# Two-tensor GpSimd instructions cut into pieces of 256 columns, in a two-layer attention kernel on one core

## The chip, the core and the metric

The kernel runs on one NeuronCore of a Trainium2 chip, in one launch. Five engines work beside each other, each through its own list of instructions in order: TensorE (PE in the profile, with its weight loads as PEld), VectorE (DVE), ScalarE (ACT), GpSimd (POOL) and SyncE (SP), which here only issues DMAs. The metric is the device time of the launch in microseconds, the median over runs. One more run carried the profiler; the trace and all rows below are from that one.

## The reference

What is computed is a small transformer of two layers over 1024 image tokens of 1024 features and 256 context tokens, all in float32. The first layer has a windowed attention of 8 heads with a sink (A) and a differential attention of 4 heads (B). The second has a neighbourhood attention (D) and one with low-rank keys and values (M). Around them stand a modulated norm, the input projections with rotary position turns, a gate, the output projection and a last norm. The part that the change touches most is the differential attention, which takes the difference of two softmaxes:

```
def _diff_attend(q, k, v, lam):
    s = jnp.einsum('bqhte,bkhte->bhtqk', q, k).astype(jnp.float32) * (q.shape[-1] ** -0.5)
    p = jax.nn.softmax(s, axis=-1)
    a = (p[:, :, 0] - lam * p[:, :, 1]).astype(v.dtype)
    return jnp.einsum('bhqk,bkhe->bqhe', a, v)
...
    yb = rmsnorm(yb, b_subln_g) * (1.0 - lam_init)
```

## The kernel before

TensorE multiplies in the format float32r. To keep float32 accuracy, every operand x is held as a high part (x copied into float32r, by ScalarE) and a low part (x minus its high part), and a product is three matmuls: high by high, high by low, low by high (`mm3`, L286 to L288). The subtraction that makes a low part is one instruction with two tensors as inputs. Low parts of values that lie in PSUM, the matmul accumulator, are made by VectorE; those of values in SBUF, the working memory, mostly by GpSimd: weights (`wlo`, L233, 1024 columns each), projected heads after the rotary turn (`hl`, L212, 512 columns), the modulated input (`hE` L502, `hO` L465), the output weights (`woE`, `woO`, L823) and the gated attention output (`yl`, L841). GpSimd also does one product of the rotary turn (`rot`, L314).

The program runs through stages in this order: start (norm and first projections), e1, A (first attention, with projections of B's heads between its steps), B, outE (output projection of layer one, input of layer two), o1 (projections of layer two), D, M, outO. In stages A, B, D and M a `pipeline` weaves the steps of scores, values and norms of successive units with "fill" work, mostly projections, so that TensorE has work in between. The final order on each engine is set when the program is built, by a scheduler that places each instruction after those it depends on; the hardware then runs each engine's list in order, and semaphores hold an instruction until its inputs are there. The scheduler follows dependencies by column ranges: a reader of columns 0 to 255 waits only for what wrote these.

Stage B, where the change adds most pieces, works in units of two query blocks (i = 0, 1) of one head. For each block there are two score maps E_[0], E_[1] of 128 rows by 1280 columns (256 in a unit of context queries). VectorE brings scores from PSUM to SBUF (`evac`, L382), ScalarE takes the exponential (L888), VectorE forms a factor cc per row (L893, L894), and the mix E_[0] + cc * E_[1] is made by GpSimd for i = 0 and by VectorE for i = 1:

```
if i in POOL_MIX:
    G.tensor_scalar(E_[1][:, :ncol], E_[1][:, :ncol], cc, 1.0, ALU.mult, ALU.mult)
    G.tensor_tensor(E_[0][:, :ncol], E_[0][:, :ncol], E_[1][:, :ncol], ALU.add)
```

These are L896 and L897. TensorE then transposes the mix block by block (L927), two blocks of 128 columns to a step, and multiplies it with the values (L393 to L395). At the end of four query blocks `b_norm` normalises: a chain of small VectorE instructions of 2 or 4 columns (`evB` L959 and L960, then `rsqrt`, L188 to L201, each needing the one before), one product from PSUM (L963), and transposes back (L953, L969). Chains of the same kind stand in the other norms; stage A has a short one for its sink (`eA`, L760 to L763).

The functions that the diff touches and what calls them:

Of the kernel before, what the change touches and what calls it, by code (L numbers as in the profile page):

```python
# [96 lines left out]
def body(nc, tc, I, out, dbg=None):  # L97
# [82 lines left out]
    def f32(ap):  # L180
        return ap.bitcast(F32)
# [23 lines left out]
    def rstd_of(ss, n, width):  # L205
        v = tiny.tile([P, n], F32, tag=f"rv{n}", name="rv")
        V.tensor_scalar(v, ss, 1.0 / width, EPS, ALU.mult, ALU.add)
        return rsqrt(v, n)

    def split_to(dst_hi, dst_lo, src, psum=True):  # L210
        A.copy(dst_hi, src)  # L211
        (V if psum else lo_eng()).tensor_tensor(dst_lo, src, f32(dst_hi), ALU.subtract)  # L212

# [6 lines left out]
    class Weights:  # L220
# [5 lines left out]
        def load(self, srcs, width=D):  # L226
            hi = self.p.tile([P, self.maxk, width], F32R, tag="whi", name="whi", bufs=self.hi_bufs)
            lo = self.p.tile([P, self.maxk, width], F32R, tag="wlo", name="wlo", bufs=self.hi_bufs)
            for j, s in enumerate(srcs):
                raw = self.raw()  # L230
                SY.dma_start(raw[:, :width], s)
                A.copy(hi[:, j], raw[:, :width])  # L232
                lo_eng().tensor_tensor(lo[:, j], raw[:, :width], f32(hi[:, j]), ALU.subtract)  # L233
            return hi, lo
# [75 lines left out]
    def rope_split(tp, ps, n, cs, c0, hi, lo, rows=P):  # L310
        rot = tp.tile([P, 512], F32, tag="rot", name="rot")[:rows, :n]
        r = tp.tile([P, 512], F32, tag="rr", name="rr")[:rows, :n]
        V.stream_shuffle(rot, ps[:rows, :n], SHUF)  # L313
        G.tensor_tensor(rot, rot, cs[:rows, 1, c0:c0 + n], ALU.mult)  # L314
        V.tensor_tensor(r, ps[:rows, :n], cs[:rows, 0, c0:c0 + n], ALU.mult)
# [135 lines left out]
    def h_cols(tp, xns, layer, j, c0, h, hf_act=0, width=512):  # L451
        n = len(xns) * P
        for kt in range(NK):
# [9 lines left out]
            else:  # L463
                V.tensor_scalar(hf[:, :n], ps[:, :n], gs, sh, ALU.mult, ALU.add)
            (V if kt % 2 else G).tensor_tensor(lo, hf[:, :n], f32(hi), ALU.subtract)  # L465
            yield 0.45
# [28 lines left out]
    def shift_cols(tp, layer, j, c0, n, h):  # L495
        for kt in range(NK):
# [4 lines left out]
            A.copy(hi, hf[:, :n])  # L501
            (V if SH_V and kt % SH_V == 0 else G).tensor_tensor(lo, hf[:, :n], f32(hi), ALU.subtract)  # L502
            yield
# [311 lines left out]
    def fill_out_weights(rp, wo, src, bufs=2):  # L815
        for kt in range(NK):
            raw = rp.tile([P, D], F32, tag="wada", name="woraw", bufs=bufs)
            SY.dma_start(raw, src[:, kt * D:(kt + 1) * D])
            for c in range(2):
                cs_ = slice(c * 512, (c + 1) * 512)  # L820
                A.copy(wo[c][0][:, kt], raw[:, cs_])
                eng = V if WO_V and kt % WO_V == c else G
                eng.tensor_tensor(wo[c][1][:, kt], raw[:, cs_], f32(wo[c][0][:, kt]), ALU.subtract)  # L823
            yield WO_Y
# [8 lines left out]
    def y_part(t, src, gsrc, half, k0, k1, b):  # L833
# [6 lines left out]
        A.copy(yh[:, ks], o[:, ks])  # L840
        (V if YL_V and half == YL_V - 1 else G).tensor_tensor(yl[:, ks], o[:, ks], f32(yh[:, ks]), ALU.subtract)  # L841

# [4 lines left out]
    with ExitStack() as st:  # L847
# [4 lines left out]
        def b_scores(hd, grp, res):  # L852
# [17 lines left out]
            for i in range(2):  # L870
# [24 lines left out]
                if i in POOL_MIX:  # L895
                    G.tensor_scalar(E_[1][:, :ncol], E_[1][:, :ncol], cc, 1.0, ALU.mult, ALU.mult)  # L896
                    G.tensor_tensor(E_[0][:, :ncol], E_[0][:, :ncol], E_[1][:, :ncol], ALU.add)  # L897
                else:
# [685 lines left out]
```

## Time and profile before

| quantity | value |
|---|---|
| median of 3 runs | 1689.58 us (1688.39 to 1693.33) |
| the profiled run's own time | 1694.41 us |
| its span, first to last instruction | 1692.6 us, 1.8 us less than its time |
| TensorE matmul busy | 1599.0 us, 94% of the span |
| VectorE busy | 1117.1 us, 66% |
| ScalarE busy | 779.0 us, 46% |
| GpSimd busy | 468.1 us, 28%, in 390 instructions |
| mean granted TensorE clock | 0.986 of full speed |

Busy time of an engine is the time that its records cover. A record of VectorE or GpSimd that had to wait for a resource after it was begun counts as busy for the wait too, so that a small instruction can show a long record. The idle time in square brackets is that of the engine just before an instruction, and behind the arrow stands what ended it.

### The profile page before, as it was taken

The page shows a single profiled execution, that of the slowest core. Times are in us where ns is not written, and L with a number is a line of the kernel's source. Part 1 is how long each engine was busy: PE and PEld are TensorE (multiplying, and loading weights), DVE is VectorE, ACT ScalarE, POOL GpSimd, SP SyncE. Part 2 cuts the span into 40 slices and gives each one's busy share as a digit, 9 for nine tenths or more (in the row PEclk, how much of TensorE's full clock was granted, in tenths as well). Part 3 has the DMA queues.
Part 4 walks back from the last instruction along what each step waited for, and adds up shares of the span by engine and source line. Part 5 has one row for each costly group of instructions (what it writes and reads, how often), then busy time and mean ns, then how long its engine had stood idle before and what let it go on. Part 6 is the DMA issues. An engine that isn't in the chain of part 4 may idle for free. (4 is left out here: it accounts for less than half of the span.)

```text
span 1692.6 us, 26893 instructions
## 1 busy us (share of the span) xinstructions
PE 1599.0 (94%) x9506; PEld 1355.1 (80%) x9506; DVE 1117.1 (66%) x2964; ACT 779.0 (46%) x1590; POOL 468.1 (28%) x390
## 2 busy tenths in 40 slices
PE   6998999999999989998899999999999999999997
PEld 3687778888878778887677898889788887889886
DVE  4782229778759888887678546342676756656586
ACT  5442107666646555665333322222465645545421
POOL 0351125545433222232222102010232313322110
PEclk9999999999999999998999999999999999999999
DMA  7447773242263332223654614567865345321363
GB/s 294 168 121 229 233 223 95 82 147 82 70 210 109 101 100 97 88 76 106 208 162 155 187 58 122 156 193 227 212 172 159 104 136 187 113 82 63 101 217 100
DMA packets 157198, 242.99 MB, mean 144 GB/s; under 512 B 10348, under 2 KB 103432, under 8 KB 154376
## 3 DMA queue, kind: packets, MB, share of 16 engines
q1 hardware_dynamic: 152152, 227.91, 43.8%
q10 hardware_dynamic: 4576, 11.54, 1.8%
q0 software_dynamic: 336, 1.84, 0.3%
q8 instruction: 75, 1.23, 0.3%
q14 instruction: 59, 0.48, 0.1%
HBM read 163.50 MB, written 77.74 MB: 143 GB/s over the span
## 5 line engine op out<-in xcount | busy, mean ns | idle before, releaser
L286 PE MATMUL mmps<-hE,whi 128*128 128x512 f32 (+1 forms) x408 | 148.8, 365 | 1.7 <-DVE gg L371 1.0
L288 PE MATMUL mmps<-hE,wlo 128*128 128x512 f32 (+1 forms) x408 | 146.7, 360 | 0.0
L287 PE MATMUL mmps<-hE,whi 128*128 128x512 f32 (+1 forms) x408 | 146.1, 358 | 0.0
L888 ACT ACTIVATE sB_t<-sB_t,mB 128x1280 f32<-128x1280 f32 (+1 forms) x80 | 95.5, 1194 | 60.6 <-DVE sB_t L382 54.1
L233 POOL TENSOR_TENSOR wlo<-wraw,whi 128x1024 fp32r<-128x1024 f32 x30 | 72.2, 2406 | 182.8 <-ACT whi L232 143.9
L880 PE MATMUL sps<-kb,qb 128*128 128x512 f32 (+1 forms) x416 | 107.4, 361 | 7.1 <-DVE sB_t L382 5.8
L286 PEld LDWEIGHTS mmps<-hE,whi 128*128 128x128 f32 x408 | 77.7, 190 | 12.8 <-issue 2.5
L288 PEld LDWEIGHTS mmps<-hE,wlo 128*128 128x128 f32 x408 | 77.4, 190 | 10.3 <-issue 0.8
L382 DVE TENSOR_SCALAR_CACHE_REDUCE sB_t<-sps,mB 128x512 f32<-128x512 f32 (+1 forms) x128 | 78.1, 612 | 10.9 <-PE sps L880 8.7
L880 PEld LDWEIGHTS sps<-kb,qb 128*128 128x128 f32 x416 | 69.4, 191 | 19.1 <-DVE sB_t L382 9.7
L287 PEld LDWEIGHTS mmps<-hE,whi 128*128 128x128 f32 x408 | 77.6, 190 | 8.8
L1419 POOL TENSOR_SCALAR sM_t<-sM_t,sM 128x1280 f32<-128x1280 f32 x32 | 43.0, 1346 | 143.7 <-DVE sM L1418 112.9
L1320 POOL TENSOR_SCALAR sD_t<-sD_t,sD 128x640 f32<-128x640 f32 (+1 forms) x64 | 48.5, 780 | 104.8 <-ACT phd L211 28.6
L287 PE MATMUL mmps<-hO,whi 128*128 128x512 f32 (+1 forms) x192 | 74.9, 390 | 1.3 <-POOL hO L465 1.2
L286 PE MATMUL mmps<-hO,whi 128*128 128x512 f32 (+1 forms) x192 | 75.8, 395 | 0.0
L288 PE MATMUL mmps<-hO,wlo 128*128 128x512 f32 (+1 forms) x192 | 74.5, 388 | 0.0
L896 POOL TENSOR_SCALAR sB_t<-sB_t,cB 128x1280 f32<-128x1280 f32 (+1 forms) x20 | 23.4, 1171 | 179.8 <-DVE cB L894 66.8
L755 ACT ACTIVATE sA_t<-sA_t,mA 128x640 f32<-128x640 f32 (+2 forms) x80 | 59.6, 745 | 25.1 <-DVE sA_t L382 24.2
L765 POOL TENSOR_SCALAR sA_t<-sA_t,eA 128x640 f32<-128x640 f32 (+2 forms) x80 | 57.7, 743 | 42.1 <-DVE eA L763 23.2
L211 ACT CAST phm<-tps 128x512 fp32r<-128x512 f32 x80 | 45.7, 584 | 51.1 <-PE tps L1446 50.8
L314 POOL TENSOR_TENSOR rot<-rot,csE 128x512 f32<-128x512 f32 x26 | 36.1, 1389 | 115.6 <-DVE rot L313 100.0
L212 DVE TENSOR_TENSOR plm<-tps,phm 128x512 fp32r<-128x512 f32 x80 | 54.4, 689 | 19.5 <-ACT phm L211 19.5
(436 smaller groups left out, 5304.4 us busy)
## 6 DMA issues: line engine op xcount, KB each, us to landing
wraw<-w_e SPq DMA_DIRECT2D x26, 512.0 KB
wada<-w_ada_e SPq DMA_DIRECT2D x24, 512.0 KB
wada<-w_ada_o SPq DMA_DIRECT2D x24, 512.0 KB
wraw<-w_o SPq DMA_DIRECT2D x22, 512.0 KB
qb<-qk SPq DMA_DIRECT2D x76, 128.0 KB
qd_t<-qd SPq DMA_DIRECT2D x32, 256.0 KB
qk<-hl SPq DMA_DIRECT2D x10, 512.0 KB
vb<-vh SPq DMA_DIRECT2D x20, 256.0 KB
```

The costliest lines, as they stand in the source:

```text
L211: A.copy(dst_hi, src)
L212: (V if psum else lo_eng()).tensor_tensor(dst_lo, src, f32(dst_hi), ALU.subtract)
L233: lo_eng().tensor_tensor(lo[:, j], raw[:, :width], f32(hi[:, j]), ALU.subtract)
L286: T_.matmul(ps, lh, rh, start=first, stop=False)
L287: T_.matmul(ps, lh, rl, start=False, stop=False)
L288: T_.matmul(ps, ll, rh, start=False, stop=last)
L382: V.tensor_scalar(dst, ps, -scale, prev, ALU.mult, ALU.min, accum_out=acc)
L755: A.activation(St[:, :nl + L], St[:, :nl + L], AF.Exp, bias=mx, scale=-1.0, accum_out=ssum[:, i:i + 1])
L765: G.tensor_scalar(Ps[i][:, :nl + L], Ps[i][:, :nl + L], e[:, i:i + 1], 1.0, ALU.mult, ALU.mult)
L880: T_.matmul(ps[:, :n], Q[:, t, hl, i * P:(i + 1) * P], K[:, t, c0:c0 + n], start=hl == 0, stop=hl == 1)
L888: A.activation(St[:, :ncol], St[:, :ncol], AF.Exp, bias=mx, scale=-1.0, accum_out=s0g[:, si:si + 1] if t == 0 else ssum)
L1320: G.tensor_scalar(Ps[i][:, :w_], Ps[i][:, :w_], ssum[:, i:i + 1], 1.0, ALU.mult, ALU.mult)
```

## The change

A helper `tt` takes the place of direct two-tensor calls. For any engine but GpSimd it issues what was issued before. On GpSimd it cuts an instruction of more than 256 columns into pieces of 256 columns of the same tiles, issued one behind the other. The scale of stage B's mix on GpSimd (one tensor and a factor per row) is cut in the same way. What is computed, the engines and the buffers are the same. A GpSimd instruction of 1024 columns becomes four, one of 1280 becomes five, one of 512 two; those of 256 columns (`hO`, the context units) stay. GpSimd's list grows from 395 instructions to 718. Two two-tensor instructions that don't go through the helper (`wkr` L1103 and `xn` L1505) stay whole, and so do all one-tensor scalings of stages A, D and M (L765, L1320, L1419).

```diff
@@ -207,9 +207,19 @@
         V.tensor_scalar(v, ss, 1.0 / width, EPS, ALU.mult, ALU.add)
         return rsqrt(v, n)
 
+    def tt(eng, out_, a, b, op):
+        n, dims = out_.shape[1], len(out_.shape)
+        step = 256 if dims == 2 else 2
+        if eng is not G or n <= step:
+            eng.tensor_tensor(out_, a, b, op)
+            return
+        for c in range(0, n, step):
+            cs_ = slice(c, min(c + step, n))
+            eng.tensor_tensor(out_[:, cs_], a[:, cs_], b[:, cs_], op)
+
     def split_to(dst_hi, dst_lo, src, psum=True):
         A.copy(dst_hi, src)
-        (V if psum else lo_eng()).tensor_tensor(dst_lo, src, f32(dst_hi), ALU.subtract)
+        tt(V if psum else lo_eng(), dst_lo, src, f32(dst_hi), ALU.subtract)
 
     lo_cycle = {"n": 0, "engs": [G]}
...
@@ -311,7 +321,7 @@
         rot = tp.tile([P, 512], F32, tag="rot", name="rot")[:rows, :n]
         r = tp.tile([P, 512], F32, tag="rr", name="rr")[:rows, :n]
         V.stream_shuffle(rot, ps[:rows, :n], SHUF)
-        G.tensor_tensor(rot, rot, cs[:rows, 1, c0:c0 + n], ALU.mult)
+        tt(G, rot, rot, cs[:rows, 1, c0:c0 + n], ALU.mult)
         V.tensor_tensor(r, ps[:rows, :n], cs[:rows, 0, c0:c0 + n], ALU.mult)
         V.tensor_tensor(r, r, rot, ALU.add)
         split_to(hi, lo, r, psum=False)
...
@@ -893,8 +903,10 @@
                 V.reciprocal(cc, ssum)
                 V.scalar_tensor_tensor(cc, cc, nlam, s0g[:, si:si + 1], ALU.mult, ALU.mult)
                 if i in POOL_MIX:
-                    G.tensor_scalar(E_[1][:, :ncol], E_[1][:, :ncol], cc, 1.0, ALU.mult, ALU.mult)
-                    G.tensor_tensor(E_[0][:, :ncol], E_[0][:, :ncol], E_[1][:, :ncol], ALU.add)
+                    for c0 in range(0, ncol, 256):
+                        e1 = E_[1][:, c0:c0 + 256]
+                        G.tensor_scalar(e1, e1, cc, 1.0, ALU.mult, ALU.mult)
+                    tt(G, E_[0][:, :ncol], E_[0][:, :ncol], E_[1][:, :ncol], ALU.add)
                 else:
                     V.scalar_tensor_tensor(E_[0][:, :ncol], E_[1][:, :ncol], cc, E_[0][:, :ncol], ALU.mult, ALU.add)
                 Ps.append(E_[0])
```

The calls in `Weights.load` (L233), `h_cols` (L465), `shift_cols` (L502), `fill_out_weights` (L823) and `y_part` (L841) change in the way that the one in `rope_split` (L314) does.

The lists that come of it: on GpSimd, in the middle of stage B, a mix of a context unit (256 columns), one of a full unit, and the low part of a weight tile stand so before (`sB_t` are the score maps, `cB` the factor, `wraw` and `whi` the weight and its high part):

```order
L896 TENSOR_SCALAR sB_t<-sB_t,cB 128x256
L897 TENSOR_TENSOR sB_t<-sB_t 128x256
L896 TENSOR_SCALAR sB_t<-sB_t,cB 128x1280
L897 TENSOR_TENSOR sB_t<-sB_t 128x1280
L233 TENSOR_TENSOR wlo<-wraw,whi 128x1024
```

And so now, where lines 214 and 218 are the two calls in the helper and L908 is the scale:

```order
L908 TENSOR_SCALAR sB_t<-sB_t,cB 128x256
L214 TENSOR_TENSOR sB_t<-sB_t 128x256
L908 TENSOR_SCALAR sB_t<-sB_t,cB 128x256 x5
L218 TENSOR_TENSOR sB_t<-sB_t 128x256 x5
L218 TENSOR_TENSOR wlo<-wraw,whi 128x256 x4
```

The order of the work is the same here as everywhere on GpSimd; all five pieces of the scale come ahead of the five of the sum.

On TensorE, at the beginning of stage B, the first transposes of a full unit's mix (`tps` from `sB_t`) stand among scores (`sps`) and a projection (`mmps`) so before:

```order
L286 MATMUL mmps<-hE_134,whi 128x512
L880 MATMUL sps<-kb,qb 128x512 x2
L927 MATMUL tps<-consts,sB_t 128x128
L880 MATMUL sps<-kb,qb 128x512 x2
L927 MATMUL tps<-consts,sB_t 128x128
L287 MATMUL mmps<-hE_135,whi 128x512
```

And so now (L296, L297, L890 and L939 are the lines that were L286, L287, L880 and L927):

```order
L939 MATMUL tps<-consts,sB_t 128x128
L890 MATMUL sps<-kb,qb 128x512 x2
L939 MATMUL tps<-consts,sB_t 128x128
L296 MATMUL mmps<-hE_135,whi 128x512
L890 MATMUL sps<-kb,qb 128x512 x2
L297 MATMUL mmps<-hE_135,whi 128x512
```

The transposes stand two places earlier, since each now waits for one piece of the sum and not for all of it. Of TensorE's 9304 instructions 93 stand elsewhere than before, nearly all in this stretch at the beginning of stage B, and the lists of VectorE and ScalarE differ there and in two places of the start stage; SyncE's list is the same.

## Rows read from the trace of the kernel before

**Rows 1.** The page, busy time, share of the span and instructions of an engine.
```profile
PE 1599.0 (94%) x9506; PEld 1355.1 (80%) x9506; DVE 1117.1 (66%) x2964; ACT 779.0 (46%) x1590; POOL 468.1 (28%) x390
```

**Rows 2.** Busy us by engine in stage B (instructions), clock, DMA.
```profile
487.00:800.00 313.00, 290.96 (x1809) 251.50 (x1808) 266.74 (x822) 186.45 (x372) 89.58 (x49) 0.98 0.30 96
```

**Rows 3.** Timeline, stage B: start us, us, engine, line, operation, tiles [idle before <- releaser].
```profile
578.51 1.34 POOL L896 TENSOR_SCALAR sB_t<-sB_t,cB 128x1280 f32<-128x1280 f32 x1 [1.95 <-DVE rst L199]
579.00 0.85 DVE L200 SCALAR_TENSOR_TENSOR rst<-rst,evB 128x4 f32<-128x4 f32 x1
...
579.93 2.92 POOL L897 TENSOR_TENSOR sB_t<-sB_t 128x1280 f32<-128x1280 f32 x1
580.26 2.62 DVE L201 SCALAR_TENSOR_TENSOR rsy<-rst,rsy 128x4 f32<-128x4 f32 x1
...
584.23 0.63 PE L969 MATMUL tps<-consts,of 128*128 128x128 f32 x4 [2.18 <-DVE of L963]
```

**Rows 4.** Timeline, the last unit of stage B.
```profile
774.43 2.94 POOL L897 TENSOR_TENSOR sB_t<-sB_t 128x1280 f32<-128x1280 f32 x1
774.46 2.92 DVE L959 SCALAR_TENSOR_TENSOR evB<-s0g 128x4 f32<-128x4 f32 x1
...
779.50 0.69 PE L927 MATMUL tps<-consts,sB_t 128*128 128x128 f32 x4 [2.34 <-DVE plb L212]
```

**Rows 5.** Timeline, two more idle times of TensorE in stage B.
```profile
600.05 0.50 PE L880 MATMUL sps<-kb,qb 128*128 128x512 f32 x1 [1.96 <-DVE sB_t L382]
...
663.36 0.50 PE L880 MATMUL sps<-kb,qb 128*128 128x256 f32 x2 [1.34 <-DVE sB_t L382]
```

**Rows 6.** PE alone by stretch: start:end, us, busy (instructions), granted clock, DMA, GB/s.
```profile
585.40:588.80 3.40, 3.40 (x14) 0.51 0.38 154
...
780.00:783.40 3.40, 3.40 (x18) 0.50 0.00 0
```

**Rows 7.** GpSimd's groups by form: count | busy us, mean ns | idle before.
```profile
L233 POOL TENSOR_TENSOR wlo<-wraw,whi 128x1024 fp32r<-128x1024 f32 x30 | 72.2, 2406 | 182.8 <-ACT whi L232 143.9 <-PE sps L288 34.9 <-ACT ph L211 4.0
L897 POOL TENSOR_TENSOR sB_t<-sB_t 128x1280 f32<-128x1280 f32 x16 | 47.2, 2950 | 1.3
...
L212 POOL TENSOR_TENSOR hl<-rr,hl 128x512 fp32r<-128x512 f32 x23 | 30.8, 1339 | 23.6 <-ACT hl L211 22.1 <-DMA qd<-hl 1.5
...
L896 POOL TENSOR_SCALAR sB_t<-sB_t,cB 128x1280 f32<-128x1280 f32 x16 | 21.5, 1344 | 163.7 <-DVE cB L894 61.5 <-PE sps L880 29.1 <-ACT of L949 28.5
...
L897 POOL TENSOR_TENSOR sB_t<-sB_t 128x256 f32<-128x256 f32 x4 | 2.9, 734 | 0.3
...
L896 POOL TENSOR_SCALAR sB_t<-sB_t,cB 128x256 f32<-128x256 f32 x4 | 1.9, 480 | 16.1 <-DVE rsy L201 9.1 <-DVE cB L894 5.3 <-DVE evB L959 1.8
```

**Rows 8.** Timeline, beginning of outE: GpSimd instructions back to back.
```profile
804.93 1.69 POOL L823 TENSOR_TENSOR woE<-woraw,woE 128x512 fp32r<-128x512 f32 x1 [3.86 <-ACT woE L821]
805.39 1.26 DVE L188 TENSOR_SCALAR rsi<-evB 128x4 int32<-128x4 int32 x1
...
806.59 1.28 POOL L841 TENSOR_TENSOR yl<-o_in,yh 128x512 fp32r<-128x512 f32 x1
806.68 1.20 DVE L189 TENSOR_SCALAR rsi<-rsi 128x4 int32<-128x4 int32 x1
...
807.92 0.50 PE L288 MATMUL mmps<-woE,yl 128*128 128x512 f32 x1 [0.77 <-POOL yl L841]
```

**Rows 9.** Timeline, stage o1.
```profile
1053.87 1.90 POOL L314 TENSOR_TENSOR rot<-rot,csO 64x512 f32<-64x512 f32 x1 [3.56 <-DVE rot L313]
1054.55 4.11 DVE L315 TENSOR_TENSOR rr<-krt,csO 64x512 f32<-64x512 f32 x1
1055.73 2.38 POOL L233 TENSOR_TENSOR wlo<-wraw,whi 128x1024 fp32r<-128x1024 f32 x1
```

**Rows 10.** A VectorE line of stage A, count: duration ns min/median/max, first and last start us.
```profile
L760 DVE TENSOR_TENSOR eA<-small,mA x20: 151/162/1847, 258.1 to 461.6; 128x4 f32<-128x4 f32 x20
```

**Rows 11.** Timeline, stage o1, TensorE behind the wait of Rows 9.
```profile
1061.12 0.50 PE L286 MATMUL sps<-cq,wqk 128*128 128x512 f32 x1 [2.66 <-ACT wqk L211]
```

More of the change, by code (lines that the diff above doesn't have):

```diff
@@ L232, in load @@
                 A.copy(hi[:, j], raw[:, :width])
-                lo_eng().tensor_tensor(lo[:, j], raw[:, :width], f32(hi[:, j]), ALU.subtract)
+                tt(lo_eng(), lo[:, j], raw[:, :width], f32(hi[:, j]), ALU.subtract)
             return hi, lo
@@ L464, in h_cols @@
                 V.tensor_scalar(hf[:, :n], ps[:, :n], gs, sh, ALU.mult, ALU.add)
-            (V if kt % 2 else G).tensor_tensor(lo, hf[:, :n], f32(hi), ALU.subtract)
+            tt(V if kt % 2 else G, lo, hf[:, :n], f32(hi), ALU.subtract)
             yield 0.45
@@ L501, in shift_cols @@
             A.copy(hi, hf[:, :n])
-            (V if SH_V and kt % SH_V == 0 else G).tensor_tensor(lo, hf[:, :n], f32(hi), ALU.subtract)
+            tt(V if SH_V and kt % SH_V == 0 else G, lo, hf[:, :n], f32(hi), ALU.subtract)
             yield
@@ L822, in fill_out_weights @@
                 eng = V if WO_V and kt % WO_V == c else G
-                eng.tensor_tensor(wo[c][1][:, kt], raw[:, cs_], f32(wo[c][0][:, kt]), ALU.subtract)
+                tt(eng, wo[c][1][:, kt], raw[:, cs_], f32(wo[c][0][:, kt]), ALU.subtract)
             yield WO_Y
@@ L840, in y_part @@
         A.copy(yh[:, ks], o[:, ks])
-        (V if YL_V and half == YL_V - 1 else G).tensor_tensor(yl[:, ks], o[:, ks], f32(yh[:, ks]), ALU.subtract)
+        tt(V if YL_V and half == YL_V - 1 else G, yl[:, ks], o[:, ks], f32(yh[:, ks]), ALU.subtract)
     mark("B")
```

## The prediction

> **What bounds the kernel now.** I read the page's busy times first: TensorE's matmuls cover 94% of the span, GpSimd 28% [rows 1]. A change on GpSimd can therefore not win by shorter GpSimd work; it can only win or lose through the some 94 us in which TensorE stands idle (1692.6 - 1599.0). Second, the busy times by stretch: in stage B TensorE was busy 290.96 of 313.00 us, so 22.0 us of that idle time lie here, the most of any stage [rows 2]. Third, I went through the timeline of stage B at TensorE's longest idle times, and looked at what VectorE and GpSimd did just before.
>
> What the reader should see first is a pattern of ends. A GpSimd scale of 1.34 us runs from 578.51 to 579.85, and `rst` of L200, 4 columns wide, has a record that ends at 579.85 also. The sum L897 runs from 579.93 to 582.85, and L201, begun at 580.26, ends at 582.88 [rows 3]. L959 and its L897 do the same at 774.46 [rows 4]. Four columns are no work for 2.9 us: a two-input instruction of the same width on L760 has a median of 162 ns in 20, with one of 1847 [rows 10]. So a VectorE instruction that takes two operands from SBUF, or one of the `rsqrt` chain, waits for the GpSimd instruction that is running, up to its whole length. TensorE pays behind it: its idle time of 2.18 us at 584.23 ends on a VectorE result that follows L201 [rows 3], that of 2.34 us at 779.50 on one that follows L959 [rows 4], and there are more of 1.96 and 1.34 us [rows 5]. After the first two the granted clock falls to 0.51 and 0.50, the lower of the two levels (1.2 GHz), for 3.40 us each [rows 6]. In o1 the longest case stands: L315 at 1054.55 takes 4.11 us, through the rest of `rot` and a whole `wlo` [rows 9], and TensorE then is idle for 2.66 us [rows 11].
>
> **The change part by part. The cost on GpSimd.** A two-tensor piece of 256 columns takes 734 ns, a scale piece 480 ns (L897 and L896 in the context units) [rows 7]. From the counts and means of the same group: `wlo` 30 x (4 x 734 - 2406) = 15.9 us (33 such, with three tiles of the start, by this estimate 17); the sum of the mix 16 x (5 x 734 - 2950) = 11.5; its scale 16 x (5 x 480 - 1344) = 16.9; the instructions of 512 columns (the 23 `hl`, and `rot`, `yl`, `woE`, `woO`, `hE`: some 100) at 2 x 734 - 1339 = 0.13 each, 13. Together about 59 us, so GpSimd goes from 468 to some 527 us, 31%. I cost them at nothing on the path, except where TensorE waits for GpSimd, because GpSimd was idle 182.8 us before `wlo`s and 163.7 before scales, waiting for its inputs [rows 7]. That cover is gone at the beginning of outE, where `woE` and `yl` come back to back and TensorE waits 0.77 us for `yl` [rows 8]; some eight pieces in such chains at 0.13 each make 1.0 us more, between 0 and 3.
>
> **The mix.** All five scales now come ahead of five sums: the first piece of the mix is ready after 5 x 0.48 + 0.73 = 3.1 us instead of 1.34 + 2.95 = 4.3, the last after 6.1. TensorE takes two blocks of 128 columns, one piece, to a transpose step, and other matmuls stand between the steps; so the first step can start 1.2 us earlier, and the last is 1.8 us late but several steps away. I take 0 for it, between -3 and +5 (the 16 full mixes, a quarter of 1.2 us gained or 0.3 us lost each).
>
> **What VectorE gets back.** The trace has no train of pieces, but it has GpSimd instructions back to back with VectorE at their boundary: `rsi` of L188 waits for `woE` to 806.62, ends at 806.65 and L189 is begun at 806.68, though `yl` follows at 806.59. Then L189 waits out `yl` to 807.87 [rows 8]. So one waiting instruction gets through at each boundary, and the next waits again. A wait that was up to 2.95 us becomes one of at most one piece, 0.73. A chain of single instructions can however pay a piece per link. From the four idle times of stage B:
> - 584.23: L201 waits 0.73 at most and not 2.62, which is 1.89 less of an idle time of 2.18. I take 1.9.
> - 779.50: L959 the same, 2.92 - 0.73 = 2.19; but it is the head of a chain whose next links fall into the train, now 0.7 us longer. I take 1.5.
> - 1.96 and 1.34 us [rows 5]: half of each, 1.0 and 0.7, since chains follow there too.
>
> That is 5.1 us of 7.8. The other 14.2 us of idle time in B (22.0 - 7.8) are many short ones; some end on the mix or on a VectorE instruction behind GpSimd and some on neither. I take a quarter, 3.5 us, between 0 and a half. The two stretches of low clock cost half of their 3.4 us, 1.7 each, as the same matmuls would take half at the full clock; if the idle time ahead goes, the stretch should go. Three quarters of it: 2.5. In stage A, L760 with its worst of 1847 ns is the head of the short chain: I take 1.0 for the twenty. In o1, L315 would wait for one piece instead of a piece and a `wlo`: of 2.66 us of idle time 1.5, between 0 and all. Start, e1, D, M, outE and outO I put at 0: their GpSimd instructions are of 256 columns already, or not cut, or stand beside DMA waits. A VectorE instruction that now runs sooner can hold GpSimd up in turn: `woE` with 1.69 us beside the mean of 1.34 for 512 columns shows that it waits as well [rows 7, 8]; this is in the 1.0 above.
>
> Sum: -5.1 - 3.5 - 2.5 - 1.0 - 1.5 + 1.0 = -12.6 us. The profiled execution took 1694.41 us (span 1692.6 and 1.8 around it), so it would take 1681.8; it was 4.8 us above the median of 1689.58. On the median the sum gives 1677.0.
>
> What the Trainium skill says of this wait points the same way for a single instruction and leaves the train open. "SBUF — State Buffer", section "Who interferes with whom", gives VectorE and GpSimd one pair of ports under an exclusive lock; who issues first keeps it for its whole instruction, and a VectorE instruction with two SBUF inputs needs it. The trace agrees: 2.62 and 2.92 us of waiting to the end of an L897 [rows 3, 4].
>
> **Rivals.**
> *The train holds on as one.* If the next piece is begun before the one in hand has wholly ended, VectorE may not get in between. For it speaks L315: it was begun at 1054.55 during `rot`, and did not get in when `wlo` was begun at 1055.73, with `rot` ending at 1055.77 [rows 9]. Against it speak the boundary at 806.62 [rows 8] and that between L896 and L897, where L200 ended [rows 3]; in those, all tiles have 128 partitions, as all pieces of the mix and of `wlo` have, where `rot` in o1 has 64. If it holds, a wait lasts for the train: each of the 16 sums ends 0.72 us later (3.67 instead of 2.95), each `wlo` 0.53. If all 16 reach TensorE, 16 x 0.72 = 11.5 us are lost: 1701. It decides from the point at which a small instruction beside a mix lasts over 2.95 us.
> The Trainium skill has the rule that would bring it about: "GPSIMD Engine Reference", section "2.1 Instruction dispatch", says that consecutive GpSimd instructions are no barrier between its cores, each of which starts its share of the next as soon as it is through with the last. By that rule the ports would never be quite free inside a train; the boundary at 806.62 does not bear that out for 128 partitions.
>
> *A piece per link, no net change.* In a chain of a dozen dependent small instructions each waits for one piece. Then only the first wait shrinks, the train is 0.7 us longer, and the end of the chain is where it was. For it: L188 and L189 paid 1.26 and 1.20 us one after the other [rows 8]. Against it: at 580 only L201 stood behind the sum, the last link before the product [rows 3]. The gains at 584 and of o1 alone (1.9 + 1.5) less 1.0 and 2 lost in longer trains give -0.4: 1689.
>
> *Half comes back.* The waits shrink, but TensorE meets the next late thing, the exponentials or a DMA of `qb`, within the same step, and the clock stays as it is: 12.6 less 2.5 for the clock and half the rest, about -5: 1684.
>
> *The change does nothing to the order.* On TensorE only 93 instructions stand elsewhere, so a better or worse order by itself is no case here.
>
> **How the numbers follow.** Chances: the forecast (-8 to -20) 0.60; half comes back 0.15; no net change 0.17; the train holds 0.08. The time predicted is 1677. Within 0.3% (5 us), which is about what a measurement of this kernel can tell from no change, lie 1684.5 to 1694.6. Faster: 0.60 and half of "half comes back", 0.68. Same: the other half, 0.07, and 0.13 of "no net change", 0.20. Slower: 0.04 and 0.08, 0.12. Low end: all of the four idle times (7.8), half of the other 14.2, both stretches (3.4), 2.7 in o1 and 2 in A, 23 us: 1666. High end: 1691, which holds "no net change" and leaves the train out, and the worse part of the mix.
>
> **What would show it.** In the profile after: the records of L959, L201 and their like no longer than 0.9 us; GpSimd busy some 527 us; TensorE's idle time in B near 11 us instead of 22; clock at 1.0 where 585.4 and 780.0 stood; the krt product in o1 (L315) at some 1.5 us. It is wrong if small VectorE records last 3 us and more beside a mix (the train), if they come in rows of 0.7 with the idle times where they were (a piece per link), or if TensorE's waits for GpSimd at outE grow by more than 3 us.

## The result, and the profile after

The changed kernel takes 1678.63 us (median of 7 runs, 1673.38 to 1683.13), the kernel before 1697.79 us (7 runs, 1688.39 to 1708.29). The ratio is 0.990, interval 0.987 to 0.993: 1.0% or some 17 us faster. The forecast was 1677.0 us, 12.6 less than the median then known (1689.58). With the runs taken since, that median is 8.2 us higher, so the difference is the fairer measure of the forecast than the time: 12.6 us forecast, some 17 measured. The profiled span fell from 1692.6 to 1671.6 us; this execution took 1673.38 us, the fastest of the seven and 5.2 us below their median, so that differences between profiles come out larger than the change is.

First line of the page of the changed kernel, to be set beside [rows 1]:

```profile
PE 1592.2 (95%) x9506; PEld 1347.9 (81%) x9506; DVE 1083.9 (65%) x2964; ACT 778.5 (47%) x1590; POOL 537.6 (32%) x713
```

GpSimd is 69.5 us busier, VectorE 33.2 us less with the same 2964 records: those 33 us were waits inside records. TensorE does the same 9506 matmuls in 6.8 us less, at a mean granted clock of 0.990 instead of 0.986, and idles 14.2 us less (93.6 to 79.4).

To see where, I cut both traces at the same matmuls. These are five stages of the changed kernel (start, A, B, o1, M): start:end, us, then busy us of PE, PEld, DVE, ACT and POOL (instructions), clock, DMA share, GB/s.

```profile
0.00:142.40 142.40, 118.42 (x657) 86.08 (x657) 87.29 (x162) 64.45 (x109) 56.49 (x64) 0.95 0.53 182
...
260.30:487.50 227.20, 225.85 (x1336) 194.92 (x1335) 173.91 (x522) 143.49 (x330) 121.03 (x171) 1.00 0.37 117
487.50:790.00 302.50, 285.99 (x1809) 246.39 (x1807) 255.72 (x821) 186.40 (x371) 117.31 (x194) 1.00 0.31 99
...
949.80:1189.00 239.20, 235.24 (x1387) 210.08 (x1387) 104.36 (x281) 67.90 (x147) 35.27 (x45) 1.00 0.55 164
...
1385.90:1578.80 192.90, 188.03 (x1274) 168.52 (x1273) 125.73 (x317) 104.01 (x172) 59.23 (x52) 1.00 0.32 104
```

The same for a second profile of the kernel before, taken later to see what a stage varies by with nothing changed:

```profile
0.00:141.00 141.00, 118.20 (x656) 86.02 (x656) 93.00 (x162) 64.16 (x109) 48.13 (x37) 0.95 0.54 184
...
260.70:489.70 229.00, 225.64 (x1335) 194.81 (x1334) 176.53 (x522) 143.58 (x330) 114.23 (x120) 1.00 0.37 116
489.70:801.40 311.70, 290.18 (x1808) 250.37 (x1807) 266.50 (x821) 186.07 (x371) 89.36 (x48) 0.98 0.30 96
...
960.10:1205.40 245.30, 238.48 (x1386) 212.54 (x1385) 108.56 (x281) 68.03 (x147) 29.49 (x19) 0.99 0.54 159
...
1405.20:1601.30 196.10, 189.79 (x1274) 169.99 (x1273) 127.94 (x317) 104.03 (x172) 56.49 (x42) 0.99 0.30 100
```

Against this second profile B gains 9.2 us (10.4 against the first, cut at the same matmuls), o1 6.1, M 3.2 (5.2 against the first), A 1.8, and the start loses 1.4 (3.6 against the first). Not all of this is the change. In the kernels further down that have the changed kernel's text of o1 and M, o1 takes 239.2 to 242.5 us, which is below the 244.9 and 245.3 of the two profiles of before, but M takes 192.9 to 197.1, so M's 3.2 to 5.2 us are not clear of noise. TensorE's idle time in B, span less busy time, went from 21.5 to 16.5 us.

The waits themselves. Duration ns min/median/max of three small VectorE lines in the changed kernel (L201 of `rsqrt`, L770 the former L760, and the second `evB`, L972):

```profile
L201 DVE SCALAR_TENSOR_TENSOR rsy<-rst,rsi x30: 149/161/736, 12.0 to 1026.6; 128x2 f32<-128x2 f32 x20, 128x4 f32<-128x4 f32 x10
```
```profile
L770 DVE TENSOR_TENSOR eA<-small,mA x20: 150/162/656, 260.2 to 462.1; 128x4 f32<-128x4 f32 x20
```
```profile
L972 DVE SCALAR_TENSOR_TENSOR evB<-ssB,evB x12: 152/156/1071, 510.7 to 794.8; 128x4 f32<-128x4 f32 x8, 128x2 f32<-128x2 f32 x4
```

Where maxima were 2.62 and 2.92 us [rows 3, 4] and 1847 ns [rows 10], they are now a piece, 0.74 us at most. The exceptions are L199 once beside `wkr`, which stays whole (1.27 us), and L972, which comes back below. In o1 the wait of 4.11 us at L315, now L325, is 1.23, and TensorE's idle time behind it 0.94 instead of 2.66 [rows 9, 11]. Timeline of the changed kernel there:

```profile
1041.92 2.50 POOL L218 TENSOR_TENSOR rot<-rot,csO 64x256 f32<-64x256 f32 x2 [3.55 <-DVE rot L323]
...
1042.60 1.23 DVE L325 TENSOR_TENSOR rr<-krt,csO 64x512 f32<-64x512 f32 x1
...
1047.35 0.50 PE L296 MATMUL sps<-cq,wqk 128*128 128x512 f32 x1 [0.94 <-ACT wqk L221]
```

### The profile page after: what moved, and what is told of

Read it like the earlier page. It is cut to its first block, busy times and chain, and to the rows that moved or that the text cites. A ratio compares the mean times of both kernels' runs of the same rounds, so it can differ in the third digit from the quotient of the medians.

```text
span 1671.6 us, 27299 instructions
## 1 busy us (share of the span) xinstructions
PE 1592.2 (95%) x9506; PEld 1347.9 (81%) x9506; DVE 1083.9 (65%) x2964; ACT 778.5 (47%) x1590; POOL 537.6 (32%) x713
## 3 DMA queue, kind: packets, MB, share of 16 engines
q8 instruction: 75, 1.23, 0.3%
## 5 line engine op out<-in xcount | busy, mean ns | idle before, releaser
L296 PE MATMUL mmps<-hE,whi 128*128 128x512 f32 (+1 forms) x408 | 148.3, 364 | 2.0 <-DVE gg L381 1.3
L297 PE MATMUL mmps<-hE,whi 128*128 128x512 f32 (+1 forms) x408 | 145.7, 357 | 0.3 <-POOL hE L218 0.3
L218 POOL TENSOR_TENSOR wlo<-wraw,whi 128x256 fp32r<-128x256 f32 x120 | 90.2, 783 | 172.9 <-ACT whi L242 137.7
L890 PE MATMUL sps<-kb,qb 128*128 128x512 f32 (+1 forms) x416 | 106.9, 358 | 4.1 <-DMA kb<-kb 2.3
L908 POOL TENSOR_SCALAR sB_t<-sB_t,cB 128x256 f32<-128x256 f32 x84 | 38.6, 478 | 154.6 <-DVE cB L904 74.5
L296 PEld LDWEIGHTS mmps<-hE,whi 128*128 128x128 f32 x408 | 77.2, 189 | 12.9 <-issue 2.5
L392 DVE TENSOR_SCALAR_CACHE_REDUCE sB_t<-sps,mB 128x512 f32<-128x512 f32 (+1 forms) x128 | 78.3, 613 | 12.3 <-PE sps L890 9.7
L297 PEld LDWEIGHTS mmps<-hE,whi 128*128 128x128 f32 x408 | 77.0, 189 | 9.4 <-POOL hE L218 0.7
L890 PEld LDWEIGHTS sps<-kb,qb 128*128 128x128 f32 x416 | 68.8, 189 | 16.1 <-DVE sB_t L392 5.2
L297 PE MATMUL mmps<-hO,whi 128*128 128x512 f32 (+1 forms) x192 | 74.9, 390 | 1.7 <-POOL hO L214 1.6
L218 POOL TENSOR_TENSOR rot<-rot,csE 128x256 f32<-128x256 f32 x52 | 41.5, 819 | 108.2 <-DVE rot L323 93.3
L296 PE MATMUL mmps<-hO,whi 128*128 128x512 f32 (+1 forms) x192 | 75.9, 395 | 0.0
L298 PE MATMUL mmps<-hO,wlo 128*128 128x512 f32 (+1 forms) x192 | 74.5, 388 | 0.0
L765 ACT ACTIVATE sA_t<-sA_t,mA 128x640 f32<-128x640 f32 (+2 forms) x80 | 59.6, 746 | 25.6 <-DVE sA_t L392 24.8
L218 POOL TENSOR_TENSOR yl<-o_in,yh 128x256 fp32r<-128x256 f32 x36 | 30.9, 878 | 125.2 <-ACT yh L850 125.2
```

Of the source, the lines that this page charges most:

```text
L218: eng.tensor_tensor(out_[:, cs_], a[:, cs_], b[:, cs_], op)
L296: T_.matmul(ps, lh, rh, start=first, stop=False)
L297: T_.matmul(ps, lh, rl, start=False, stop=False)
L298: T_.matmul(ps, ll, rh, start=False, stop=last)
L392: V.tensor_scalar(dst, ps, -scale, prev, ALU.mult, ALU.min, accum_out=acc)
L765: A.activation(St[:, :nl + L], St[:, :nl + L], AF.Exp, bias=mx, scale=-1.0, accum_out=ssum[:, i:i + 1])
```

## The experiments

**The mix alone, and all but the mix.** The first cuts only the mix:

```diff
-        if eng is not G or n <= step:
+        if True:
...
-                    tt(G, E_[0][:, :ncol], E_[0][:, :ncol], E_[1][:, :ncol], ALU.add)
+                    for c0 in range(0, ncol, 256):
+                        e0, e1 = E_[0][:, c0:c0 + 256], E_[1][:, c0:c0 + 256]
+                        G.tensor_tensor(e0, e0, e1, ALU.add)
```

The second cuts all but the mix:

```diff
-                    for c0 in range(0, ncol, 256):
-                        e1 = E_[1][:, c0:c0 + 256]
-                        G.tensor_scalar(e1, e1, cc, 1.0, ALU.mult, ALU.mult)
-                    tt(G, E_[0][:, :ncol], E_[0][:, :ncol], E_[1][:, :ncol], ALU.add)
+                    G.tensor_scalar(E_[1][:, :ncol], E_[1][:, :ncol], cc, 1.0, ALU.mult, ALU.mult)
+                    G.tensor_tensor(E_[0][:, :ncol], E_[0][:, :ncol], E_[1][:, :ncol], ALU.add)
```

> Only the mix of stage B is cut (scale and sum in pieces of 256); all other GpSimd instructions are whole as before. Theory (VectorE waits for a running GpSimd instruction to its end, and shorter pieces shorten that wait): the 10.4 us that the changed kernel gained in B stay for the most part, the 5.8 us of o1 and 5.2 us of M go, the start loses nothing: 8 to 10 us under the kernel before, ratio 0.994 to 0.996; no VectorE instruction beside a mix above 0.9 us, but L315 in o1 near 4 us again and those beside a weight's low part near 2.4. Rival (the mix is ready by pieces, so that transposes start earlier): the same in B, ratio 0.994. This run doesn't tell the two apart; it sizes the mix against the rest.

> All is cut but the mix, whose scale and sum are whole as before. Theory of the VectorE waits: the sums of 2.95 us hold VectorE again, with records of 2.5 to 2.9 us in B, TensorE's idle time in B between 18 and 22 us; o1 and M keep their gains: 6 to 10 us under the kernel before, ratio 0.994 to 0.996. Rival (readiness of the mix by pieces is what pays): B back at 22 us idle, and no gain at the places where only VectorE waited, ratio 0.998 to 1.0.

Measured: mix alone 0.9972 (0.9956 to 0.9988), all but the mix 0.9936 (0.9915 to 0.9957). Together 0.9908, the whole change's 0.990: the parts add up, and the mix is the smaller. The mix alone fell short of its forecast (0.994 to 0.996); all but the mix did slightly better than its own, which was the same. Stage B in the two, same columns:

```profile
490.50:803.20 312.70, 291.61 (x1808) 251.67 (x1807) 261.24 (x821) 186.21 (x371) 114.51 (x176) 0.98 0.30 96
```
```profile
488.10:792.90 304.80, 286.15 (x1809) 246.40 (x1808) 262.87 (x821) 185.66 (x370) 93.77 (x66) 1.00 0.31 98
```

With the mix alone, B is as long as before, though VectorE's records shrank by some 5 us, so this profile doesn't show where the 0.28% comes from. The timeline of that kernel shows one reason: a small VectorE record that waits not for one piece but to the end of all five (512.34 + 3.50 = 515.84), and TensorE idle behind it.

```profile
512.34 3.50 POOL L911 TENSOR_TENSOR sB_t<-sB_t 128x256 f32<-128x256 f32 x5
513.68 2.17 DVE L974 SCALAR_TENSOR_TENSOR evB<-ssB,evB 128x2 f32<-128x2 f32 x1
...
516.51 0.90 PE L890 MATMUL sps<-kb,qb 128*128 128x256 f32 x3 [1.84 <-DVE sB_t L392]
```

Without the mix's cut B is 7 to 8 us shorter than in the two profiles of before, and 4 to 5 of that is TensorE's busy time. Its idle time of 2.20 us behind a whole sum is still there, and yet the clock stayed at 1.00, the upper level, behind it. First the timeline, then PE by stretch (busy us, clock, DMA share, GB/s):

```profile
580.17 2.63 DVE L201 SCALAR_TENSOR_TENSOR rsy<-rst,rsy 128x4 f32<-128x4 f32 x1
...
584.16 0.63 PE L979 MATMUL tps<-consts,of 128*128 128x128 f32 x4 [2.20 <-DVE of L973]
```
```profile
583.80:587.20 3.40, 3.04 (x21) 1.00 0.65 188
587.20:590.60 3.40, 3.40 (x25) 1.00 0.13 52
```

**The kernel before once more.**

> The kernel before, profiled a second time, to see what a stage and a low-clock stretch vary by with nothing changed. If the low clock behind the idle times at 582 and 777 us belongs to them, it is there again, and stage B takes 312 to 314 us; if it falls by chance, the idle times are there again to 0.1 us and the low clock is not, and B takes 306 to 312 us.

It took 1695.73 us. The four idle times of [rows 3 to 5] are there again within 0.02 us. Behind that of 2.35 us the low clock is there again too (0.50 from 783.3), but behind that of 2.17 us no low stretch follows; one comes 15 us later, behind that of 1.95 us, where the first profile had none. Timeline, then PE by stretch:

```profile
587.10 0.63 PE L969 MATMUL tps<-consts,of 128*128 128x128 f32 x4 [2.17 <-DVE of L963]
```
```profile
587.10:590.50 3.40, 3.40 (x23) 1.00 0.36 145
602.40:605.80 3.40, 3.40 (x14) 0.50 0.36 94
```

So an idle time of 2 us does not always bring the lower clock, and 1.7 us of a profile's gain in one place may be this and no more.

**Pieces of the mix in the other order, and pieces of 512.** The first (here its scale; the sum has the same loop), then the second:

```diff
-                    for c0 in range(0, ncol, 256):
+                    for c0 in reversed(range(0, ncol, 256)):
```
```diff
-        step = 256 if dims == 2 else 2
+        step = 512 if dims == 2 else 4
...
-                    for c0 in range(0, ncol, 256):
-                        e1 = E_[1][:, c0:c0 + 256]
+                    for c0 in range(0, ncol, 512):
+                        e1 = E_[1][:, c0:min(c0 + 512, ncol)]
```

> As the changed kernel, but the five pieces of the scale and of the sum are issued from the last columns to the first, so that the first transposes of a unit wait for the last piece. VectorE's waits are as short as in the changed kernel. Theory of the VectorE waits: the gain stays, ratio 0.990 to 0.992, TensorE's idle time in B 16 to 18 us. Rival (readiness by pieces): the first transposes wait for the whole train, 6.1 us instead of 4.3 before; B's idle time back at 20 us or more, ratio 0.995 to 0.998.

> Pieces of 512 columns instead of 256 everywhere (1280 becomes 512, 512 and 256; 1024 becomes two; the 512 ones stay whole). GpSimd busy near 490 us. Theory of the VectorE waits: a wait is at most 1.34 us, in between 0.74 and 2.95; the gain is a half to three quarters of the changed kernel's, ratio 0.992 to 0.995, longest small VectorE record in B 1.3 us. Rival (any cut of a mix frees the first transposes): about the same as the changed kernel, since the first piece of the mix is ready after 3.0 us in both, ratio 0.990.

Measured: 0.9941 (0.9923 to 0.9958) and 0.9930 (0.9914 to 0.9946). Stage B, last columns first, then pieces of 512:

```profile
486.70:792.40 305.70, 289.77 (x1809) 249.00 (x1808) 255.73 (x821) 185.92 (x371) 120.02 (x194) 0.99 0.31 98
```
```profile
488.40:792.70 304.30, 287.54 (x1808) 247.63 (x1807) 258.24 (x821) 186.49 (x371) 101.76 (x117) 0.99 0.31 98
```

With the last columns first, TensorE's idle time in B is 15.9 us, as low as in the changed kernel, so it is not the early first piece that shortens it: the rival of readiness expected 20 or more. But the ratio lies between the two forecasts (0.990 to 0.992 and 0.995 to 0.998), nearer to the rival's; part of the difference stands outside B (D took 202.6 us there, 196.9 in the changed kernel), where the two kernels have the same text. D took 196.9 and 199.8 us in the two profiles of before, so half of this can come with nothing changed. Pieces of 512 keep some two thirds of the gain, as the theory of waits has it, though their interval overlaps the changed kernel's, and TensorE's idle time in B is 16.8 us, about as low as there; small VectorE records in B go up to 1.23 us there.

**The weights' low parts whole.**

```diff
-        if eng is not G or n <= step:
+        if eng is not G or n <= step or n == 1024:
```

> The changed kernel with the low parts of weight tiles (wlo, 1024 columns, 33 of them) whole again. The cut of all but the mix had brought 0.64%, that of the mix alone 0.28%; this says whether the wlo are the larger part. If waits behind wlo are: ratio 0.994 to 0.996, L315 near 4 us again, o1 back near 244 us and B near 306. If the pieces of 512-column instructions (hl, rot, yl, woE, woO) are: ratio 0.990 to 0.992 as the changed kernel.

Measured: 0.9976 (0.9957 to 0.9995), less gain than expected. The instructions of 1024 columns alone are worth some 0.7% of the 1.0% (0.9976 against 0.990, each with an interval of 0.2 to 0.3% to either side). They are the `wlo` only: the two `ws` of 1024 columns (2.39 us each) don't go through the helper either, and stay whole in every kernel here. The lists of TensorE, VectorE and ScalarE are the changed kernel's, and in neither kernel does an idle time of TensorE end on a `wlo`, so it is not that a low part is ready by pieces. Stage B there:

```profile
490.40:798.30 307.90, 288.70 (x1808) 248.94 (x1807) 259.53 (x821) 186.48 (x372) 115.16 (x179) 0.99 0.30 97
```

o1 is 243.0 us, L325 takes 4.25 us once more, and TensorE is idle behind it for 2.91.

**The four idle times, run by run.** Two things differ in the lists of these kernels. Where the pieces of the mix begin at the first columns (mix alone, pieces of 512, low parts whole, the changed kernel), TensorE's transposes stand early at the beginning of B; all but the mix and last columns first have the order of before there. From 560 us to the end of B, TensorE, VectorE and ScalarE run the same lists in all of them, so that the four idle times of [rows 3 to 5] can be looked up at the same matmul:

| before | mix alone | all but the mix | last columns first | low parts whole | changed |
|---|---|---|---|---|---|
| 2.18 at 584.23 | 0 | 2.20 | 0 | 0 | 0 |
| 2.34 at 779.50 | 0 | 2.35 | 0 | 0 | 0 |
| 1.96 at 600.05 | 0.11 | 1.96 | 0.10 | 0.10 | 0.10 |
| 1.34 at 663.36 | 1.34 | 0 | 0 | 1.34 | 0 |

Three go where the mix is cut, from whichever end, and stay where it is whole; the fourth goes with the cut of the low parts. So these idle times belong to the length of the instruction that VectorE waited for. For the time of the whole kernel it shows less: last columns first and all but the mix have the same lists on all three engines, differ in the mix alone, and take the same time (0.9941 and 0.9936). The gain of the mix is seen only in kernels that also have the early transposes; how much of it is their order and how much the shorter waits, no run here tells apart.

**An idle sum on GpSimd, whole and in pieces.** Behind each of the 16 full mixes one more sum that nobody reads; first into the spent map, then into a tile of its own:

```diff
+                    if ncol > 256:
+                        G.tensor_tensor(E_[1], E_[1], E_[1], ALU.add)
```
```diff
+                    if ncol > 256:
+                        G.tensor_tensor(junk, E_[0], E_[0], ALU.add)
```

and each with `tt(G, ...)` in its place. All engines' lists but GpSimd's are the changed kernel's.

> The changed kernel, and behind each full mix of stage B one more two-tensor instruction of 1280 columns on GpSimd, whole, whose result nobody reads (it doubles the spent score map in place): 16 more instructions of 2.95 us, 47 us. Nothing becomes ready earlier or later by it but the spent buffer, so it shows the price of a whole instruction as a bystander. Theory of the VectorE waits: small VectorE records of up to 2.9 us in B again, and 4 to 10 us over the changed kernel, ratio to the kernel before 0.994 to 0.997. Rival (what counts is when the mix is ready, and waits of small VectorE instructions are hidden): as the changed kernel, 0.989 to 0.992.

> The same idle instruction as five pieces of 256 columns (some 59 us of GpSimd). Theory of the VectorE waits: a bystander in pieces costs little, no small VectorE record above 0.75 us, 0 to 3 us over the changed kernel, ratio 0.990 to 0.992, and faster than the whole one by 3 to 8 us. Rival of the train (pieces hold VectorE as one): as slow as the whole one or slower, 0.995 to 0.998. Rival of readiness: both like the changed kernel.

> The changed kernel with an idle sum of 1280 columns on GpSimd behind each full mix of stage B, whole, into a tile of its own: it reads the finished mix, which the transposes hold anyway, so that the spent score map is given back as early as in the changed kernel (the earlier idle sums had written that map, and cost 32 and 43 us). All other engines' lists are those of the changed kernel. Theory now: the early idle sums cost what they did because the score map came free some 2.3 to 3.5 us later in each unit; then this one is far cheaper, and what it costs is the price of VectorE's waits: 2 to 9 us over the changed kernel, ratio to the kernel before 0.992 to 0.996, with small VectorE records up to 2.4 us in B. Rival (GpSimd's list itself is the bound in B, and any work on it is paid for): 25 to 35 us over the changed kernel, 1.004 to 1.01.

> The same idle sum in five pieces; all lists but GpSimd's are the same as in the whole one. Theory of the VectorE waits: no small VectorE record above 0.75 us, and 2 to 6 us faster than the whole one, ratio 0.989 to 0.993. Rival that a chain pays a piece per link, so that whole and pieces cost the same: within 2 us of the whole one. Rival of GpSimd's list as the bound: slower than the whole one by some 10 us, as with the earlier pair.

Measured, in this order: 1.0096 (1.0072 to 1.0120), 1.0171 (1.0145 to 1.0197), 1.0028 (1.0008 to 1.0048), 1.0078 (1.0051 to 1.0106). All my figures were too low, and in both pairs the pieces are the slower: the expectation that VectorE would get in between them fell. Stage B of the four:

```profile
488.30:828.00 339.70, 304.58 (x1808) 264.44 (x1807) 270.99 (x821) 187.64 (x372) 157.29 (x210) 0.93 0.27 88
```
```profile
485.90:837.30 351.40, 304.81 (x1809) 263.75 (x1808) 281.98 (x821) 186.78 (x370) 163.04 (x274) 0.92 0.26 85
```
```profile
486.10:807.40 321.30, 292.44 (x1809) 252.04 (x1808) 270.69 (x821) 186.35 (x370) 157.88 (x210) 0.98 0.30 93
```
```profile
487.80:823.70 335.90, 300.42 (x1809) 258.98 (x1808) 280.59 (x821) 186.80 (x371) 166.47 (x274) 0.94 0.28 89
```

The tile of its own saves 18.4 us whole and 15.5 in pieces: that much of the first pair's cost I put down to the score map that came free later, since the lists are the same and only the tile differs. What is left for a whole bystander, 18.8 us over the changed kernel's B (12.3 idle, 6.5 busy, by the same rows), is more than twice the 2 to 9 us that I had expected, and less than the 25 to 35 of the rival that GpSimd's list is the bound. The trace speaks against that rival: in B none of the idle times before TensorE's matmuls ended on GpSimd, and GpSimd was still idle for 67.1 us before scales whose factor wasn't there (74.5 in the changed kernel). VectorE's records in B grew by 15.0 us over the changed kernel's with the same list. The longest waits have the expected form, a small VectorE record of the bystander's length and TensorE idle behind it:

```profile
513.23 2.32 POOL L912 TENSOR_TENSOR junkP<-sB_t 128x1280 f32<-128x1280 f32 x1
513.33 2.24 DVE L188 TENSOR_SCALAR rsi<-evB 128x2 int32<-128x2 int32 x1
...
516.31 0.63 PE L942 MATMUL tps<-consts,sB_t 128*128 128x128 f32 x4 [2.11 <-DVE rsi L189]
```

In pieces VectorE's records grew by 24.9 us, and the 8.5 us that this kernel is slower than the whole one are close to the rival's 10. Here the factor cc of one instruction waited for nine of them, through two trains (717.24 + 5.24 = 722.48; 719.68 + 2.79 = 722.47), and TensorE was idle for 4.28 us:

```profile
716.83 2.90 POOL L218 TENSOR_TENSOR junkP<-sB_t 128x256 f32<-128x256 f32 x5
...
717.24 5.24 DVE L905 SCALAR_TENSOR_TENSOR cB<-cB,nlam,s0g 128x1 f32<-128x1 f32 x1
...
719.68 2.79 POOL L218 TENSOR_TENSOR wlo<-wraw,whi 128x256 fp32r<-128x256 f32 x4
...
725.14 0.79 PE L891 MATMUL sps<-kb,qb 128*128 128x256 f32 x2 [4.28 <-DVE sB_t L392]
```

**Eight score maps, and the scale of M in pieces.** The second has both edits:

```diff
-S_BUFS_A, S_BUFS_B, S_BUFS_D, S_BUFS_M, K_BUFS_B, Q_BUFS_B = 11, 7, 12, 6, 1, 3
+S_BUFS_A, S_BUFS_B, S_BUFS_D, S_BUFS_M, K_BUFS_B, Q_BUFS_B = 11, 8, 12, 6, 1, 3
```
```diff
-                G.tensor_scalar(St, St, ssum, 1.0, ALU.mult, ALU.mult)
+                for c0 in range(0, St.shape[1], 256):
+                    G.tensor_scalar(St[:, c0:c0 + 256], St[:, c0:c0 + 256], ssum, 1.0, ALU.mult, ALU.mult)
```

> The changed kernel with eight buffers for the score maps of stage B instead of seven. Theory that part of the mix's gain is given back because the longer train frees the spent map later: VectorE's waits for GpSimd before bringing in scores (6.5 us in 6 cases in the changed kernel, 0.7 in one before) go, and the time falls by 2 to 5 us, ratio 0.986 to 0.990. Rival (these waits are hidden): as the changed kernel, 0.989 to 0.992.

> The one before, and the scale of stage M (1280 columns, one tensor, 32 of them, whole so far) in pieces of 256 too, which adds 32 x (5 x 0.48 - 1.34) = 34 us of GpSimd work. Theory of the VectorE waits: the 1.63 us that VectorE's low part of woO takes beside such a scale falls under 1.2, M loses 1 us of idle time: 0 to 2 us faster than the one before. Rival (one-tensor pieces cost more than they free, as each map of M is given to the transposes 1.1 us later): 1 to 4 us slower.

Measured: 0.9881 (0.9847 to 0.9915) and 0.9895 (0.9866 to 0.9924). B falls to 300.8 us with eight maps:

```profile
486.20:787.00 300.80, 287.07 (x1809) 246.95 (x1808) 256.17 (x821) 186.16 (x371) 117.75 (x194) 0.99 0.32 100
```

TensorE's idle time there is 13.7 us, against 16.5; its list stands in another order there, too. Neither time can be told from the changed kernel's 0.990, nor from each other. It can't be said that either version beats it.

## Why the prediction was right, point by point

**The bound and the sign** were right: TensorE's idle time behind VectorE's waits was the lever, and GpSimd's 69.5 us more (59 forecast) cost little. At outE, where I had put 1.0 us, TensorE's idle times that ended on GpSimd grew from 3.4 us to 4.2, though the stage is no longer than before (159.8 us now, 160.1 and 158.7 before). The sum of 59 was low. A piece of `wlo` has a median of 740 ns but a mean of 783, with some up to 1.72 us, which I read as GpSimd waiting for VectorE in turn; groups of GpSimd in the changed kernel, mean ns behind the busy us:

```profile
L218 POOL TENSOR_TENSOR wlo<-wraw,whi 128x256 fp32r<-128x256 f32 x120 | 90.2, 783 | 172.9 <-ACT whi L242 137.7 <-PE sps L298 31.2 <-ACT ph L221 4.0
L218 POOL TENSOR_TENSOR sB_t<-sB_t 128x256 f32<-128x256 f32 x80 | 57.5, 754 | 0.0
```

where 734 was taken [rows 7].

**The four idle times of B**, -5.1: the mechanism was right, and the term too small. All four went, 7.7 us of 7.8 (the table above). These are the matmuls that had 2.18 and 2.34 us of idle time before them in [rows 3, 4], in the changed kernel, where the view has no idle time to show:

```profile
582.04 0.60 PE L981 MATMUL tps<-consts,of 128*128 128x128 f32 x4
...
772.64 0.63 PE L939 MATMUL tps<-consts,sB_t 128*128 128x128 f32 x4
```

**The other idle times of B**, -3.5, failed: they did not shrink but grew by 2 to 3 us, since all of B's idle time fell by 5.0 to 5.5 us only (from 21.5 and 22.0 to 16.5). New idle times stand before matmuls that waited for nothing before. The longest:

```profile
770.83 3.52 POOL L218 TENSOR_TENSOR sB_t<-sB_t 128x256 f32<-128x256 f32 x5
...
773.30 1.07 DVE L972 SCALAR_TENSOR_TENSOR evB<-ssB,evB 128x4 f32<-128x4 f32 x1 [0.41 <-ACT junkb L969]
...
776.33 1.55 DVE L911 SCALAR_TENSOR_TENSOR sB_t<-sB_t,cB 128x1280 f32<-128x1280 f32 x1
...
778.70 0.63 PE L939 MATMUL tps<-consts,sB_t 128*128 128x128 f32 x4 [2.70 <-DVE plb L214]
```

L972, the head of a chain, is held to the end of the train; VectorE then works through the chain, the factor and its own mix of 1.55 us without a pause of note, and `plb` stands behind them. For the 0.7 us that L972 was held beyond the piece in hand, this is the rival of the train. One of 2.28 us stands at 546.30: TensorE reaches the scores of the next head before their `kb` has landed. On VectorE's side of that place each link of the chain pays a piece, here the first two of four:

```profile
540.48 3.52 POOL L218 TENSOR_TENSOR sB_t<-sB_t 128x256 f32<-128x256 f32 x5
541.28 0.67 DVE L188 TENSOR_SCALAR rsi<-evB 128x4 int32<-128x4 int32 x1
541.98 0.66 DVE L189 TENSOR_SCALAR rsi<-rsi 128x4 int32<-128x4 int32 x1
...
546.30 0.36 PE L890 MATMUL sps<-kb,qb 128*128 128x256 f32 x1 [2.28 <-DMA kb<-kb]
```

So a piece per link is real where a chain meets a train, but TensorE waited for the DMA there. A new idle time of 1.49 us has its reason in the mix. The rival that half comes back, as TensorE meets the next late thing, described B's idle time better than my quarter did. The 11 us named as a sign was a slip besides: 22.0 less the 8.6 of these two terms is 13.4, and the clock's 2.5 is busy time.

**The mix at 0** was wrong by its side effect. Five pieces of a scale and of a sum take longer than the two whole ones (3.52 us for the sum, 2.95 before), and the map they read is given back later. VectorE's waits in B that ended on a piece of GpSimd's sum, us, times, longest us:

```profile
DVE sB_t L392 <- POOL sB_t L218: 4.6, 3, 1.9
```

Before, one wait of 0.7 us was all, and one of 0.7 us is there still. The expectation for eight maps has 6.5 us in 6 cases, which counts waits of TensorE's weight loads in. With eight maps VectorE's waits for GpSimd in B are gone, as that expectation had it. TensorE paid for the longest of the three:

```profile
597.03 0.69 DVE L392 TENSOR_SCALAR_CACHE_REDUCE sB_t<-sps 128x512 f32<-128x512 f32 x1 [1.88 <-POOL sB_t L218]
...
599.88 0.39 PE L405 MATMUL pvps<-plb,vbt 128*128 128x256 f32 x1 [1.49 <-DVE plb L214]
```

I had weighed only who reads the mix, not who waits for its buffer.

**Where the gain lies** was mis-sized: I gave most of the sum to waits behind L897; the mix alone brings 0.28%, the weights' low parts some 0.7%. In o1 TensorE's idle time fell by 2.5 to 2.9 us where I had 1.5, and its busy time by 3.2 where I had none; A gave 1.8 us where I had 1.0. That the total is near 12.6 is therefore partly luck, errors that cancel: some 3 us too much in B's idle time, and too little in the clock and o1.

**The clock**, -2.5: at 584 and 780 the low stretches are gone, and B's busy time is 4.2 to 4.9 us less. But all but the mix lost them too with the idle times still there, so this term has the right sign and no proven cause. It was priced for B alone; in o1 both profiles of before have two stretches at 0.50, of which the changed kernel has none (its clock in o1 is 1.00).

**The train as one** was held at 0.08 and came true in one case of twenty. Over thirteen traces, one of the kernel before among them, I counted 988 VectorE records held by a GpSimd instruction with another right behind it: 939 ended with the one that held them, 49 later. Of these, 17 were begun in its last 0.11 us; of the other 32, 17 are the factor cc and 11 the second `evB`, held up to 5.5 us. The changed kernel has two, of 0.64 and 0.92 us, so the rival cost little there; the bystander in pieces met it ten times and the whole one twice, which goes with the 8.5 us between them. The Trainium skill's "GPSIMD Engine Reference", section "2.1 Instruction dispatch", says that consecutive GpSimd instructions are no barrier between its cores. Taken, as in the prediction, to mean that nothing gets in inside a train, it is not borne out by the 939; the 49 show that a boundary is no promise either.

## What to carry to other kernels

Where one engine's small instructions wait out another's long ones, the length of the long ones sets the wait: look for small records that end when a long one elsewhere ends, and cut that one, first where it stands beside a chain on the critical path. Ask of every instruction made longer by it which buffer it gives back later, and what is late next once the wait is gone. An instruction that nobody needs, put in whole and in pieces with all other lists the same, shows what such a wait costs apart from when a result is ready, and showed here that cutting can also lose. And follow each idle time at the same matmul: here all four that were aimed at went, and others came in their place.

## What the runs showed of the hardware that was not expected

A VectorE instruction is not always let in between two GpSimd instructions: L905 waited 5.24 us through nine pieces, while in trains of the same kernel L188, L189, L199 and L200 got in at each boundary, and L201 at all but one, 0.10 us before which it was begun. Why `cB<-cB,nlam,s0g` and `evB<-ssB,evB` are the ones left out no run here shows; `evB<-s0g`, the line before, of the same shape, got in 69 times of 69. Of the two, others of the same line got in, 18 and 22 times. And the same idle time of TensorE was followed by a granted clock of 0.51 in one profile of the kernel before (2.18 us) and by 1.00 in the other (2.17 us).
